# A first projection group on rows that are not yet normed

## The chip, the cores and the metric

The kernel runs on one core of one Trainium2 chip. Its metric is the device time of one execution in microseconds (us). A core has five engines that run side by side, each through its own instructions in order: TensorE (PE, matrix products into PSUM), VectorE (DVE), ScalarE (ACT), GpSimd (POOL) and SyncE (SP, which here only issues transfers). They wait for each other by semaphores. Weights and inputs come from HBM by DMA.

## The reference

Two transformer blocks on 256 tokens of width 2048, in float32. The first is a conformer convolution block with an MLP, the second mixes two kinds of attention and has an MLP of its own. The change lies in the first lines of the first block:

```python
def rms_norm(x, g):
    xf = x.astype(jnp.float32)
    y = xf * lax.rsqrt(jnp.mean(xf * xf, axis=-1, keepdims=True) + NORM_EPS)
    return (y * g.astype(jnp.float32)).astype(x.dtype)

def conformer_conv(h, w_pw1, b_pw1, w_dw, b_dw, ln_g, ln_b, w_pw2, b_pw2):
    u = h @ w_pw1 + b_pw1                       # h = rms_norm(x, norm_mix_g), 2048 -> 4096
    a, gate = jnp.split(u, 2, axis=-1)
    u = a * jax.nn.sigmoid(gate)
    u = depthwise_conv(u, w_dw) + b_dw          # 31 taps along the tokens, one filter per channel
    u = jax.nn.silu(layer_norm(u, ln_g, ln_b))
    return u @ w_pw2 + b_pw2

h = x + conformer_conv(rms_norm(x, norm_mix_g), ...)
h = h + square(relu(rms_norm(h, norm_ffn_g) @ w_up)) @ w_down
h = rms_norm(h, final_norm_g)
# second block: rmsnorm, projections, stick-breaking and forgetting attention, output
# projection, rmsnorm, squared-relu MLP, final rmsnorm
```

1/rms is one number per token, so it can stand ahead of the projection or behind it: (r * x * g) @ W is r * ((x * g) @ W).

## The kernel before

**Exact products.** Every float32 operand of a matrix product is split into `hi`, a rounded copy that TensorE takes at its fast rate, and `lo`, the rest. A product is hi*hi + hi*lo + lo*hi. For weights, `split(i)` has ScalarE cast `raw` to `hi` (L127) and VectorE or GpSimd subtract to get `lo` (L128): VectorE for steps 0 to 4, GpSimd for later projection steps. For activations `split_act` does the same (L178, L179).

**Steps.** The program is a list of steps, one unit of weights of 1 MB each. `emit` writes them out in order: for step i it first issues loads (three units ahead, three `raw` buffers) and splits (one unit ahead up to step 2, two ahead from step 3 on), then the step's matmuls, and then whatever earlier steps have deferred by a number of steps (`run_pending`). For the first 40 steps the order so written is the order of every engine's queue.

**Stage 1.** The pointwise projection goes in groups of two channel blocks (`groups`), for each of which a step takes a quarter of the 2048 inputs: steps 0 to 3 are group 0 with quarters kq = 0 to 3, steps 4 to 7 group 1, and so on. A step has 48 matmuls into the PSUM tile `pw` (L518, L520, L521). The activations of quarter kq are the tile `xa[kq]`: 4 blocks of 128 channels, hi and lo, 256 tokens. The same four tiles serve all groups. Behind the last quarter `glu` gates the result (ScalarE's sigmoid `sg`, VectorE's product `u_p`, ScalarE's copy `u`), and `conv(gi)` is deferred so that it comes behind the first step of the next group: some of the 31 taps of each channel block on TensorE (`ca`, with diagonal matrices `dg` that ScalarE makes), the others on VectorE, 54 multiply-adds for group 0 (L394), the sum into `xs_t` (L406). Layer norm follows after all groups.

**The start.** `prologue` loads x into `res` (two tiles of 128 tokens), has ScalarE square it (L208) and takes 1/rms (`rstd_of`). Quarter c of x, here chunk c, then goes through `first_a` (ScalarE and VectorE multiply by 1/rms into `xn`, TensorE transposes into `pt`) and `first_b` (VectorE multiplies by the gain into `xf`, L307; `split_act` into `xa[c]`), both called from `split`. `vectors`, in step 2, transposes the small vectors and the filters.

Of the kernel before, what the change touches and what calls it, by code (L numbers as in the profile page):

```python
# [10 lines left out]
AF = mybir.ActivationFunctionType  # L11
# [4 lines left out]
P = 128  # L16
# [17 lines left out]
def kernel(  # L34
# [31 lines left out]

    state = {}

# [1 line left out]
    ident = const.tile([P, P], F32, name="ident")  # L70
    ones = const.tile([P, P], F32, name="ones")
    ones_c = const.tile([P, P], F32, name="ones_c")
# [17 lines left out]
        nc.scalar.dma_start(out=t, in_=bass.AP(tensor=v.tensor, offset=v.offset, ap=[[0, P], [1, D]]))  # L90
        return t

# [1 line left out]
    steps = []  # L94

    def unit_std(w, r0, c0):
# [15 lines left out]
    def split(i):  # L112
        if callable(steps[i][0]):
            parts[i] = steps[i][0]()
            return
        srcs, eng = steps[i][0]
        if i < 4:
            for c in ((0, 1), (), (2,), (3,))[i]:
                first_a(c)
            first_b(i)  # L120
        raw = raws.pop(i)
        hi = wpool.tile([P, D], F32R, tag="hi", name=f"hi{i}")
        lo = wpool.tile([P, D], F32R, tag="lo", name=f"lo{i}")
        e = nc.gpsimd if eng == "p" and i > 4 else nc.vector
        n = D if i else D // 2
        for j in range(0, D, n):
            nc.scalar.copy(hi[:, j:j + n], raw[:, j:j + n])  # L127
            e.tensor_tensor(out=lo[:, j:j + n], in0=raw[:, j:j + n], in1=hi[:, j:j + n].bitcast(F32), op=ALU.subtract)  # L128
        k = srcs[0][0]
        parts[i] = (hi.rearrange("p (k c) -> p k c", k=k), lo.rearrange("p (k c) -> p k c", k=k))  # L130

# [41 lines left out]

    mm = nc.tensor.matmul

# [1 line left out]
    def split_act(src, hi, lo):  # L177
        nc.scalar.copy(hi, src)  # L178
        nc.vector.tensor_tensor(out=lo, in0=src, in1=hi.bitcast(F32), op=ALU.subtract)  # L179
# [52 lines left out]
                mm(ps[h], xh, lo[:, k, :], start=False, stop=False)  # L232
                mm(ps[h], xl, hi[:, k, :], start=False, stop=(last and k == 3))  # L233

# [1 line left out]
    s1 = ExitStack()  # L236
    p1 = s1.enter_context(tc.tile_pool(name="stage1", bufs=1))
    cpool = s1.enter_context(tc.tile_pool(name="cpool", bufs=4))
# [1 line left out]
    def prologue():  # L240
        nc.vector.memset(col[:, 0:1], 1.0)
        nc.vector.memset(col[:, 1:2], EPS1)
        nc.vector.memset(col[:, 2:3], EPS2)
        nc.vector.memset(col[:, 3:4], 0.0)
        nc.scalar.preload_act_table_set(LOG_EXP)
        for h in range(2):
            for j in range(2):
                nc.sync.dma_start(out=res[:, h, j * 1024:(j + 1) * 1024],
                                  in_=x[h * P:(h + 1) * P, j * 1024:(j + 1) * 1024])
        make_identity(nc, ident)  # L250
        vab = xpool.tile([P, 3, P], F32, tag="xt", name="vab")
        va, vb, vm = (vab[:, i, :] for i in range(3))
        wdr = xpool.tile([P, D], F32, tag="xt", name="wdr")[0:KT, :]
        nc.scalar.dma_start(out=vm[0:16, :], in_=norm_mix_g.rearrange("(k p) -> k p", p=P))
        for i, g in enumerate((norm_ffn_g, g_attn, g_mlp, final_norm_g, b_dw, ln_g, ln_b)):
            nc.gpsimd.dma_start(out=va[16 * i:16 * i + 16, :], in_=g.rearrange("(k p) -> k p", p=P))
        nc.gpsimd.dma_start(out=vb[0:32, :], in_=b_pw1.rearrange("(k p) -> k p", p=P))
        nc.gpsimd.dma_start(out=vb[32:40, :], in_=g_out_sb.rearrange("(k p) -> k p", p=P))
        nc.gpsimd.dma_start(out=vb[40:48, :], in_=g_out_fox.rearrange("(k p) -> k p", p=P))
        nc.gpsimd.dma_start(out=wdr, in_=w_dw)  # L260
        state["raw_vectors"] = va, vb, wdr
        ss0 = new_ss("ss0")
        for h in range(2):
            for j in range(2):
                for c in range(2):
                    sumsq(ss0, h, 2 * j + c)
        r = rstd_of(ss0, EPS1, "r0")
        state["r0"], state["xa"] = r, [xt_tile(f"xa{c}") for c in range(4)]
        pm = ps1([P, 16], "pm")
        nc.tensor.transpose(pm, vm[0:16, :], ident[0:16, 0:16])  # L270
        nc.vector.tensor_copy(vt[:, G_MIX:G_MIX + 16], pm)
        nc.vector.memset(ones, 1.0)
# [11 lines left out]
                nc.tensor.transpose(pw[:, k, 0:KT], wdr[:, cb * P:(cb + 1) * P], ident[:KT, :KT])  # L284
            nc.vector.tensor_copy(wd[:, 8 * q:8 * q + 8, 0:KT], pw[:, :, 0:KT])

    def first_a(c):
        r, pts = state["r0"], []
        for h in range(2):
            xn = wk([P, 512], "xn")  # L290
            src = res[:, h, c * 512:(c + 1) * 512]
            if h == 0:
                nc.scalar.activation(out=xn, in_=src, func=AF.Copy, scale=r[:, h:h + 1])
            else:
                nc.vector.tensor_scalar(out=xn, in0=src, scalar1=r[:, h:h + 1], scalar2=None, op0=ALU.mult)
            pt = ps1([P, 4, P], f"pt{h}{c}")
            for k in range(4):
                nc.tensor.transpose(pt[:, k, :], xn[:, k * P:(k + 1) * P], ident)
            pts.append(pt)
        state["pts", c] = pts  # L300

    def first_b(c):
        g = vt[:, G_MIX + 4 * c:G_MIX + 4 * c + 4].unsqueeze(2).to_broadcast([P, 4, P])
        xfs, xt = [], state["xa"][c]
        for h, pt in enumerate(state.pop(("pts", c))):
            xf = wk([P, 4, P], "xf")
            nc.vector.tensor_tensor(out=xf, in0=pt, in1=g, op=ALU.mult)  # L307
            xfs.append(xf)
        for h, xf in enumerate(xfs):
            split_act(xf, xt[:, :, 0, h * P:(h + 1) * P], xt[:, :, 1, h * P:(h + 1) * P])  # L310

    def late_constants():
        rowbc = bcast_rows(b_pw2, "bpw2")
# [16 lines left out]
        for h in range(2):  # L330
            nc.gpsimd.tensor_tensor(out=res[:, h, :], in0=res[:, h, :], in1=rowbc, op=ALU.add)

# [1 line left out]
    xs_t = p1.tile([P, NB, T], F32, name="xs_t")  # L334
    u_t = [p1.tile([P, 2, T + 2 * PAD], F32, name=f"u{i}") for i in range(2)]
    acc0 = p1.tile([P, T], F32, name="acc0")
# [6 lines left out]
    def glu(gi, ps):  # L343
        cbs = groups[gi]
        u = u_t[gi % 2]
        state["u_p", gi] = []
        for i, cb in enumerate(cbs):
            sg = wk([P, T], "sg")
            nc.scalar.activation(out=sg, in_=ps[:, 2 + i, :], func=AF.Sigmoid, bias=vcol(B_PW1, 16 + cb))
            up = ps1([P, 512], "u_p")  # L350
            nc.vector.memset(up[:, 0:PAD], 0.0)
            nc.vector.memset(up[:, T + PAD:T + 2 * PAD], 0.0)
            nc.vector.scalar_tensor_tensor(out=up[:, PAD:PAD + T], in0=ps[:, i, :], scalar=vcol(B_PW1, cb),
                                           in1=sg, op0=ALU.add, op1=ALU.mult)
            nc.scalar.copy(u[:, i, PAD:PAD + T], up[:, PAD:PAD + T])
            state["u_p", gi].append(up)
# [138 lines left out]
    def stage1_group(gi):  # L495
        cbs = groups[gi]
        if len(cbs) == 2:
            for kq in range(4):
                c0 = cbs[0] * P
                unit = ([(4, 512, 0, w_pw1[kq * 512:(kq + 1) * 512, c0:c0 + 256]),  # L500
                         (4, 512, 256, w_pw1[kq * 512:(kq + 1) * 512, D + c0:D + c0 + 256])], "p")

                def fn(hi, lo, kq=kq):
                    if kq == 0:
                        state["pw1"] = ps2([P, 4, T], f"pw1_{gi}")
                    if gi == 0 and kq == 2:
                        vectors()
                    if kq == (3 if gi == 0 else 0):
                        state["dg", gi] = diags(gi)
                    if gi == 1 and kq == 0:  # L510
                        late_constants()
                    ps, xt = state["pw1"], state["xa"][kq]
                    for m in range(4):
                        for k in range(4):
                            wh, wl = hi[:, k, m * P:(m + 1) * P], lo[:, k, m * P:(m + 1) * P]
                            first = kq == 0 and k == 0
                            last = kq == 3 and k == 3
                            mm(ps[:, m, :], wh, xt[:, k, 0, :], start=first and m % 2 == 0, stop=False,  # L518
                               skip_group_check=True)
                            mm(ps[:, m, :], wh, xt[:, k, 1, :], start=False, stop=False, skip_group_check=True)  # L520
                            mm(ps[:, m, :], wl, xt[:, k, 0, :], start=False, stop=last, skip_group_check=True)  # L521
                    if kq == 3:
                        glu(gi, ps)
                        defer(2, lambda: conv(gi))
                step(unit, fn)
# [34 lines left out]
                            add_bias_rows()  # L560
                step(unit, fn)

# [1 line left out]
    def post_chunk(c, ss, gain, xts, delay):  # L564
        for h in range(2):
            sumsq(ss, h, c)
# [40 lines left out]
            srcs, _ = unit_std(w_pw2, q * 512, c * 512)  # L607
            step((srcs, "p" if q == 0 and c < 2 or (q, c) == (1, 0) else "v"), fn)

# [1 line left out]
    def ffn(w_u, w_d, tail):  # L611
        NG = FF // 512

# [78 lines left out]
            defer(2, spread)  # L692
        defer(1, rate)

# [1 line left out]
    s2 = ExitStack()  # L696

    def open_attention():
# [70 lines left out]
        state["lr"] = lr  # L769

    def attention(kind, grp, qk, v, mt):
        """Four heads: list of steps, each emitted in order with the projections between."""
        ap = state["ap"]
        qT, kT = qk
        per_pair = []
# [196 lines left out]
                eng = nc.sync if j == 0 else nc.scalar  # L972
                eng.dma_start(out=out[h * P:(h + 1) * P, j * 1024:(j + 1) * 1024], in_=v)

# [1 line left out]
    for gi in range(len(groups)):  # L976
        stage1_group(gi)
    pw2()
# [54 lines left out]
```

## Time and profile before

| | |
|---|---|
| median of 3 runs | 2202.88 us (2202.71 to 2204.14) |
| span of the profiled execution | 2200.8 us |
| TensorE busy | 2166.2 us, 98% of the span |
| VectorE, ScalarE, GpSimd busy | 65%, 44%, 8% |
| read from HBM | 391.53 MB |

The profiled execution has no time of its own beside its span, which goes from its first to its last instruction; the runs' times are 2.1 us above it (median). In the profile L127 is line 127 of the kernel; `PE` is TensorE's matmuls, `PEld` its weight loads; a group of instructions is written as line, engine, operation, `out<-in` and shape. `[0.86 <-PE pw L521]` is the idle time ahead of an instruction on its engine and what ended it. A row of a stretch gives its start and end, its length, the busy time and count of each engine, the granted share of TensorE's clock, the DMA share and GB/s.

### The profile page before, as it was taken

To read this page: it belongs to the slowest core of one execution; us is meant where nothing else is said; L and a number is where in the kernel's file an instruction comes from. 1 tells how busy PE (TensorE), PEld (TensorE's weight loads), DVE (VectorE), ACT (ScalarE), POOL (GpSimd) and SP (SyncE) were. 2 spreads that over 40 slices of the span, in tenths; PEclk is the share of its full clock that TensorE was granted. 3 is DMA by queue.
4 is the path that set the end of the run, shared out by engine and by line. 5 is a ranking of instruction groups with operands and counts; after the bars stand their busy time and mean duration, and the time that the engine had idled before them with its cause. 6 is when DMAs were issued, how large, how long until landed. Compare 5 with 4: busy or idle time off the path is not lost.

```text
span 2200.8 us, 27600 instructions
## 1 busy us (share of the span) xinstructions
PE 2166.2 (98%) x11521; PEld 1861.1 (85%) x11521; DVE 1436.8 (65%) x1648; ACT 958.8 (44%) x965; POOL 175.2 (8%) x88
## 2 busy tenths in 40 slices
PE   7999899999999999999999999999999999999998
PEld 7999778888888888888788888888888888888886
DVE  5997775666655666566866565676656665666656
ACT  6455454434333433343645454544333433343333
POOL 2886500000000000000000000000000000000000
PEclk9999999999999999999999999999999999999999
DMA  7555155555555555556544554455555555555553
GB/s 227 164 170 150 63 193 187 186 188 188 190 191 191 184 198 191 191 174 221 177 156 153 172 172 159 166 172 191 192 189 187 186 190 189 191 189 192 191 191 134
DMA packets 219612, 395.41 MB, mean 180 GB/s; under 512 B 8993, under 2 KB 46017, under 8 KB 219073
## 3 DMA queue, kind: packets, MB, share of 16 engines
q1 hardware_dynamic: 216160, 389.05, 54.6%
q10 hardware_dynamic: 2960, 4.27, 0.6%
q8 instruction: 90, 1.47, 0.3%
q0 software_dynamic: 368, 0.34, 0.1%
q14 instruction: 34, 0.28, 0.0%
HBM read 391.53 MB, written 2.10 MB: 179 GB/s over the span
## 4 chain that ended last, share of the span: by engine, by line
PE 97%; ACT 1%; DVE 1%; issue 0%; DMA 0%; ACTq 0%; SPq 0%; DVEq 0%
PE up L222 22%; PE dn L231 11%; PE dn L233 11%; PE dn L232 11%; PE up L224 10%; PE pj L222 5%; PE pj L224 3%; PE pw L521 2%; PE pw L518 2%; PE pw L520 2%; PE ca L386 2%; PE wo L232 1%; PE wo L233 1%; PE wo L231 1%; PE pv L233 1%; PE pv L231 1%
## 5 line engine op out<-in xcount | busy, mean ns | idle before, releaser
L128 DVE TENSOR_TENSOR lo<-raw,hi 128x2048 fp32r<-128x2048 f32 (+1 forms) x339 | 774.3, 2285 | 585.6 <-ACT hi L127 585.6
L127 ACT CAST hi<-raw 128x2048 fp32r<-128x2048 f32 (+1 forms) x369 | 702.8, 1906 | 935.9 <-PE up L222 340.3
L222 PE MATMUL up<-xn,hi 128*128 128x512 f32 x2048 | 718.3, 398 | 0.0
L224 PE MATMUL up<-xn,lo 128*128 128x256 f32 x1920 | 539.4, 281 | 0.0
L222 PEld LDWEIGHTS up<-xn,hi 128*128 128x128 f32 x2048 | 378.2, 188 | 83.8
L231 PE MATMUL dn<-hi,act 128*128 128x512 f32 x1024 | 398.8, 389 | 0.0
L233 PE MATMUL dn<-hi,act 128*128 128x512 f32 x1024 | 398.4, 389 | 0.0
L232 PE MATMUL dn<-lo,act 128*128 128x512 f32 x1024 | 398.3, 389 | 0.0
L224 PEld LDWEIGHTS up<-xn,lo 128*128 128x128 f32 x1920 | 362.5, 189 | 5.9
L641 DVE SCALAR_TENSOR_TENSOR res<-dn,rsq,res 128x512 f32<-128x512 f32 x256 | 191.4, 748 | 57.9 <-PE dn L233 57.9
L232 PEld LDWEIGHTS dn<-lo,act 128*128 128x128 f32 x1024 | 192.3, 188 | 40.1
L233 PEld LDWEIGHTS dn<-hi,act 128*128 128x128 f32 x1024 | 192.2, 188 | 40.1
L231 PEld LDWEIGHTS dn<-hi,act 128*128 128x128 f32 x1024 | 192.2, 188 | 38.6
L222 PE MATMUL pj<-xn,hi 128*128 128x512 f32 x512 | 179.7, 398 | 0.0
L394 DVE SCALAR_TENSOR_TENSOR acc<-u_p,wd,acc 128x256 f32<-128x256 f32 x385 | 151.6, 478 | 0.0
L128 POOL TENSOR_TENSOR lo<-raw,hi 128x2048 fp32r<-128x2048 f32 x30 | 138.5, 4620 | 85.6 <-ACT hi L127 85.6
L224 PE MATMUL pj<-xn,lo 128*128 128x256 f32 x480 | 134.5, 280 | 0.0
L518 PE MATMUL pw<-xa,hi 128*128 128x256 f32 x448 | 129.1, 288 | 0.7 <-ACT hi L127 0.7
L521 PE MATMUL pw<-xa,lo 128*128 128x256 f32 x448 | 127.6, 285 | 0.9 <-DVE lo L128 0.9
L520 PE MATMUL pw<-xa,hi 128*128 128x256 f32 x448 | 127.5, 285 | 0.0
L222 PEld LDWEIGHTS pj<-xn,hi 128*128 128x128 f32 x512 | 94.5, 188 | 20.6 <-DVE q_t L906 0.5
L224 PEld LDWEIGHTS pj<-xn,lo 128*128 128x128 f32 x480 | 90.6, 189 | 1.5
(259 smaller groups left out, 2033.5 us busy)
## 6 DMA issues: line engine op xcount, KB each, us to landing
raw<-in_ffn_w_up_dram SPq DMA_DIRECT2D x64, 1024.0 KB, 5.2
raw<-in_ffn_w_down_dram SPq DMA_DIRECT2D x64, 1024.0 KB, 5.1
raw<-in_w_up_dram SPq DMA_DIRECT2D x64, 1024.0 KB, 5.3
raw<-in_w_down_dram SPq DMA_DIRECT2D x64, 1024.0 KB, 5.0
raw<-in_w_in_dram SPq DMA_DIRECT2D x48, 1024.0 KB, 5.1
raw<-in_conv_w_pw_dram SPq DMA_DIRECT2D x64, 512.0 KB, 4.8
raw<-in_conv_w_pw_dram SPq DMA_DIRECT2D x16, 1024.0 KB, 5.1
raw<-in_w_out_dram SPq DMA_DIRECT2D x16, 1024.0 KB, 5.1
```

The costliest lines, as they stand in the source:

```text
L127: nc.scalar.copy(hi[:, j:j + n], raw[:, j:j + n])
L128: e.tensor_tensor(out=lo[:, j:j + n], in0=raw[:, j:j + n], in1=hi[:, j:j + n].bitcast(F32), op=ALU.subtract)
L222: mm(o, wh, xt[:, k, :, :], start=(kq == 0 and k == 0), stop=last)
L224: mm(o[:, 0:T], wl, xt[:, k, 0, :], start=False, stop=False, skip_group_check=True)
L231: mm(ps[h], xh, hi[:, k, :], start=(first and k == 0), stop=False)
L232: mm(ps[h], xh, lo[:, k, :], start=False, stop=False)
L233: mm(ps[h], xl, hi[:, k, :], start=False, stop=(last and k == 3))
L394: nc.vector.scalar_tensor_tensor(out=acc[k], in0=src, scalar=w, in1=acc[k], op0=ALU.mult, op1=ALU.add)
L518: mm(ps[:, m, :], wh, xt[:, k, 0, :], start=first and m % 2 == 0, stop=False, skip_group_check=True)
L520: mm(ps[:, m, :], wh, xt[:, k, 1, :], start=False, stop=False, skip_group_check=True)
L521: mm(ps[:, m, :], wl, xt[:, k, 0, :], start=False, stop=last, skip_group_check=True)
L641: nc.vector.scalar_tensor_tensor(out=r, in0=ps[h], scalar=state["rsq"][:, h:h + 1], in1=r, op0=ALU.mult, op1=ALU.add)
```

## The change

x is loaded in chunks of 512 columns, with the weights of steps 0 to 2 between them on the same queue. `first_chunk` transposes a chunk straight from `res`, multiplies by the gain into `xs_t` (which is free until conv writes it) and splits it into `xa[c]`; so `xa` holds x * g without 1/rms. Group 0 is projected on that. The sums of squares follow the weights' casts on ScalarE. After step 2 `row_scales` takes 1/rms, spreads it over the partitions by a diagonal matrix and a product with ones, and keeps it in `delta`. `glu(0)` multiplies the projection's PSUM by `delta`. For the groups after it `scale_chunk(c)`, at the head of `split(4 + c)`, multiplies the chunk in `xs_t` by `delta` and splits it into `xa[c]` again. Step 0 takes all products with `hi` ahead of those with `lo`.

```diff
@@ split
         if i < 4:
-            for c in ((0, 1), (), (2,), (3,))[i]:
-                first_a(c)
-            first_b(i)
+            first_chunk(i)
+        elif i < 8:
+            scale_chunk(i - 4)
         raw = raws.pop(i)
...
             e.tensor_tensor(out=lo[:, j:j + n], in0=raw[:, j:j + n], in1=hi[:, j:j + n].bitcast(F32), op=ALU.subtract)
+        if i < 4:
+            for h in range(2):
+                sumsq(state["ss0"], h, i)
@@ prologue
-        for h in range(2):
-            for j in range(2):
-                nc.sync.dma_start(out=res[:, h, j * 1024:(j + 1) * 1024],
-                                  in_=x[h * P:(h + 1) * P, j * 1024:(j + 1) * 1024])
+        for c in range(4):
+            for h in range(2):
+                nc.sync.dma_start(out=res[:, h, c * 512:(c + 1) * 512], in_=x[h * P:(h + 1) * P, c * 512:(c + 1) * 512])
+            if c < 3:
+                load(c)
+        at["load"] = 3
...
-        ss0 = new_ss("ss0")
-        for h in range(2):
-            for j in range(2):
-                for c in range(2):
-                    sumsq(ss0, h, 2 * j + c)
-        r = rstd_of(ss0, EPS1, "r0")
-        state["r0"], state["xa"] = r, [xt_tile(f"xa{c}") for c in range(4)]
+        state["ss0"], state["xa"] = new_ss("ss0"), [xt_tile(f"xa{c}") for c in range(4)]
@@ first_a and first_b give way to
+    def first_chunk(c):
+        g = vt[:, G_MIX + 4 * c:G_MIX + 4 * c + 4].unsqueeze(2).to_broadcast([P, 4, P])
+        xt = state["xa"][c]
+        for h in range(2):
+            pt = ps1([P, 4, P], f"pt{h}{c}")
+            for k in range(4):
+                nc.tensor.transpose(pt[:, k, :], res[:, h, (4 * c + k) * P:(4 * c + k + 1) * P], ident)
+            nc.vector.tensor_tensor(out=xs_t[:, 4 * c:4 * c + 4, h * P:(h + 1) * P], in0=pt, in1=g, op=ALU.mult)
+        for h in range(2):
+            tok = slice(h * P, (h + 1) * P)
+            split_act(xs_t[:, 4 * c:4 * c + 4, tok], xt[:, :, 0, tok], xt[:, :, 1, tok])
+
+    def row_scales():
+        r = rstd_of(state["ss0"], EPS1, "r0")
+        pr = ps1([P, T], "pr0")
+        for h in range(2):
+            dgr = wk([P, P], "dgr")
+            nc.vector.tensor_scalar(out=dgr, in0=ident, scalar1=r[:, h:h + 1], scalar2=None, op0=ALU.mult)
+            mm(pr[:, h * P:(h + 1) * P], ones, dgr, start=True, stop=True)
+        nc.scalar.copy(delta, pr)
+
+    def scale_chunk(c):
+        v = xs_t[:, 4 * c:4 * c + 4, :]
+        nc.vector.tensor_tensor(out=v, in0=v, in1=delta.unsqueeze(1).to_broadcast([P, 4, T]), op=ALU.mult)
+        xt = state["xa"][c]
+        split_act(v, xt[:, :, 0, :], xt[:, :, 1, :])
@@ glu
+        if gi == 0:
+            for m in (2, 0):
+                v = ps[:, m:m + 2, :]
+                nc.vector.tensor_tensor(out=v, in0=v, in1=delta.unsqueeze(1).to_broadcast([P, 2, T]), op=ALU.mult)
@@ stage1_group, in a step's function
+                    if gi == 0 and kq == 0:
+                        for k in range(4):
+                            for m in range(4):
+                                wh = hi[:, k, m * P:(m + 1) * P]
+                                mm(ps[:, m, :], wh, xt[:, k, 0, :], start=k == 0 and m % 2 == 0, stop=False,
+                                   skip_group_check=True)
+                                mm(ps[:, m, :], wh, xt[:, k, 1, :], start=False, stop=False, skip_group_check=True)
+                        for k in range(4):
+                            for m in range(4):
+                                mm(ps[:, m, :], lo[:, k, m * P:(m + 1) * P], xt[:, k, 0, :], start=False, stop=False,
+                                   skip_group_check=True)
+                        return
...
+                    if gi == 0 and kq == 2:
+                        row_scales()
```

What this does to the order of the queues shows at three places. First the transfers on SyncE at the start, before (`res` is x, each `raw` one unit of weights):

```order
L248 DMA res<-in_x_dram 128x1024 x4
L109 DMA raw_166<-in_conv_w_pw_dram 128x4x256 x2
L109 DMA raw_169<-in_conv_w_pw_dram 128x4x256 x2
L109 DMA raw_172<-in_conv_w_pw_dram 128x4x256 x2
L109 DMA raw_217<-in_conv_w_pw_dram 128x4x256 x2
```

and now:

```order
L251 DMA res<-in_x_dram 128x512 x2
L109 DMA raw_107<-in_conv_w_pw_dram 128x4x256 x2
L251 DMA res<-in_x_dram 128x512 x2
L109 DMA raw_112<-in_conv_w_pw_dram 128x4x256 x2
L251 DMA res<-in_x_dram 128x512 x2
L109 DMA raw_117<-in_conv_w_pw_dram 128x4x256 x2
L251 DMA res<-in_x_dram 128x512 x2
L109 DMA raw_179<-in_conv_w_pw_dram 128x4x256 x2
```

x, which came whole ahead of all weights, now comes in four parts with a unit of weights behind each.

Second, VectorE from the gate of group 0 to that of group 1, before (`u_p` the gated product, `acc` the taps of conv(0), L406 its sum):

```order
L353 SCALAR_TENSOR_TENSOR u_p<-pw_0_235,vt,sg 128x256
L399 TENSOR_SCALAR acc<-u_p,wd 128x256 x2
L394 SCALAR_TENSOR_TENSOR acc<-u_p,wd,acc 128x256 x54
L406 SCALAR_TENSOR_TENSOR xs_t<-ca_625,vt,acc 128x256 x2
L351 MEMSET u_p 128x15
L352 MEMSET u_p 128x15
L353 SCALAR_TENSOR_TENSOR u_p<-pw_1_553,vt,sg 128x256
```

and now (`xa_143` is the tile of chunk 2, `xa_144` that of chunk 3):

```order
L360 SCALAR_TENSOR_TENSOR u_p<-pw_0_209,vt,sg 128x256
L311 TENSOR_TENSOR xs_t<-xs_t,delta 128x1024
L182 TENSOR_TENSOR xa_143<-xs_t,xa_143 128x4x256
L406 TENSOR_SCALAR acc<-u_p,wd 128x256 x2
L401 SCALAR_TENSOR_TENSOR acc<-u_p,wd,acc 128x256 x54
L413 SCALAR_TENSOR_TENSOR xs_t<-ca_624,vt,acc 128x256 x2
L311 TENSOR_TENSOR xs_t<-xs_t,delta 128x1024
L182 TENSOR_TENSOR xa_144<-xs_t,xa_144 128x4x256
```

The rescaling of chunk 2 stands ahead of conv(0), that of chunk 3 behind its 58 instructions.

Third, ScalarE from the copy of `u` in group 0 to the first sigmoid of group 1, before (`hi_692` is the weights of step 7):

```order
L355 COPY u_91<-u_p 128x256
L127 CAST hi_546<-raw_387 128x2048
L367 ACTIVATE dg_554<-ident,wd 128x128 x4
L367 ACTIVATE dg_559<-ident,wd 128x128 x2
L90 DMA bpw_562<-in_conv_b_pw_dram 128x2048
L127 CAST hi_692<-raw_466 128x2048
L127 CAST hi_747<-raw_473 128x2048
```

and now (`hi_694` is the weights of step 7):

```order
L362 COPY u_91<-u_p 128x256
L181 CAST xa_143<-xs_t 128x4x256
L127 CAST hi_545<-raw_357 128x2048
L374 ACTIVATE dg_553<-ident,wd 128x128 x4
L374 ACTIVATE dg_558<-ident,wd 128x128 x2
L90 DMA bpw_561<-in_conv_b_pw_dram 128x2048
L181 CAST xa_144<-xs_t 128x4x256
L127 CAST hi_694<-raw_457 128x2048
L127 CAST hi_749<-raw_467 128x2048
```

The cast of chunk 3 stands ahead of the cast of step 7's weights; on GpSimd the order is the same in both, lo of step 7 behind those of steps 5 and 6.

More of the change, by code (lines that the diff above doesn't have):

```diff
@@ L285, in vectors @@
             nc.vector.tensor_copy(wd[:, 8 * q:8 * q + 8, 0:KT], pw[:, :, 0:KT])
-    def first_a(c):
-        r, pts = state["r0"], []
+    def first_chunk(c):
+        g = vt[:, G_MIX + 4 * c:G_MIX + 4 * c + 4].unsqueeze(2).to_broadcast([P, 4, P])
+        xt = state["xa"][c]
         for h in range(2):
[L290 to L295, printed above, removed]
             pt = ps1([P, 4, P], f"pt{h}{c}")
             for k in range(4):
[L298 to L310, printed above, removed]
+                nc.tensor.transpose(pt[:, k, :], res[:, h, (4 * c + k) * P:(4 * c + k + 1) * P], ident)
[16 more added lines that the diff above has]
+        split_act(v, xt[:, :, 0, :], xt[:, :, 1, :])
     def late_constants():
```

## The prediction

> **What bounds the kernel now.** I read the page's head and its chain of waits first, then the waits of TensorE, then the first 80 us by stretches and instruction by instruction on the engines that the change touches.
>
> ```profile
> span 2200.8 us, 27600 instructions
> PE 2166.2 (98%) x11521; PEld 1861.1 (85%) x11521; DVE 1436.8 (65%) x1648; ACT 958.8 (44%) x965; POOL 175.2 (8%) x88
> PE 97%; ACT 1%; DVE 1%; issue 0%; DMA 0%; ACTq 0%; SPq 0%; DVEq 0%
> ```
>
> TensorE is the bound almost everywhere: 34.6 us of the span are not its own. The change can win only in that remainder, so the next view is where it lies. Stretches (core, PE, PEld, DVE, ACT, POOL busy, then granted clock, DMA share, GB/s), and the waits of TensorE from 20 to 80 us:
>
> ```profile
> 0.00:5.00 5.00, 0.25 (x1) 0.18 (x1) 0.15 (x4) 1.49 (x2) 4.19 (x13) 1.00 0.61 186
> 5.00:10.00 5.00, 0.00 (x0) 0.00 (x0) 0.00 (x0) 4.34 (x13) 2.27 (x6) 1.00 1.02 329
> 10.00:15.00 5.00, 1.48 (x7) 1.48 (x8) 2.06 (x10) 2.97 (x8) 1.43 (x4) 1.00 1.11 328
> 15.00:20.00 5.00, 3.50 (x19) 2.86 (x17) 4.43 (x6) 3.13 (x4) 0.00 (x0) 1.00 0.93 275
> ...
> 17.20:20.60 3.40, 1.75 (x10) 1.34 (x11) 3.15 (x4) 1.64 (x2) 0.00 (x0) 1.00 0.69 216
> 20.60:24.00 3.40, 3.40 (x18) 3.40 (x18) 2.20 (x5) 3.08 (x4) 0.00 (x0) 0.50 0.72 219
> ...
> 56.00:73.40 17.40, 17.40 (x147) 17.40 (x146) 17.38 (x46) 4.04 (x4) 16.62 (x13) 1.00 0.58 187
> ```
> ```profile
> PE pw L521 <- DVE lo L128: 0.2, 1, 0.2
> ```
>
> The reader is to see two things. TensorE starts late: it has next to nothing until 13.5 us, and from 20.3 us (up to 80, where this view ends) it waits no more. That late start is what the change goes after. And from 56.0 to 73.4 us VectorE is busy for 17.38 of 17.40 us beside a full TensorE: VectorE has no room there either. The three steps in that stretch, 144 matmuls, give 0.12 us a matmul and 5.8 us a step of 48.
>
> The rows that set the lockstep, from the timeline (start, length):
>
> ```profile
> 47.77 0.47 ACT L349 ACTIVATE sg<-pw,vt 128x256 f32<-128x256 f32 x1 [0.86 <-PE pw L521]
> 50.35 1.02 DVE L399 TENSOR_SCALAR acc<-u_p,wd 128x256 f32<-128x256 f32 x2
> 51.28 21.24 DVE L394 SCALAR_TENSOR_TENSOR acc<-u_p,wd,acc 128x256 f32<-128x256 f32 x54
> 72.43 0.87 DVE L406 SCALAR_TENSOR_TENSOR xs_t<-ca,vt,acc 128x256 f32<-128x256 f32 x2
> 67.56 1.91 ACT L127 CAST hi<-raw 128x2048 fp32r<-128x2048 f32 x1 [3.84 <-PE pw L520]
> 73.39 0.47 ACT L349 ACTIVATE sg<-pw,vt 128x256 f32<-128x256 f32 x1 [3.92 <-PE pw L521]
> 52.72 4.60 POOL L128 TENSOR_TENSOR lo<-raw,hi 128x2048 fp32r<-128x2048 f32 x1 [4.19 <-ACT hi L127]
> ```
>
> Step 3 ends on TensorE by 47.77 us (the first sigmoid waits for it), VectorE's share of conv(0) runs from 50.35 to 73.30, 22.95 us, and step 7 ends at 73.39. VectorE and TensorE finish a group together. Whatever is put on VectorE's queue behind conv(0) and ahead of step 7 is therefore late for TensorE.
>
> **The change, part by part.** Everything is timed on the profiled execution (span 2200.8 us); the median of the runs, 2202.88, is 2.1 above that span, and I carry that over.
>
> *Start.* The transposes no longer wait for 1/rms. In the old order these rows set the start:
>
> ```profile
> 4.79 0.63 ACT L208 ACTIVATE junk<-res 128x512 f32<-128x512 f32 x1 [2.71 <-DMA res<-in_x_dram]
> 8.27 0.63 ACT L208 ACTIVATE junk<-res 128x512 f32<-128x512 f32 x1 [0.50 <-DMA res<-in_x_dram]
> 13.52 3.68 PE L298 MATMUL pt<-ident,xn 128*128 128x128 f32 x16 [9.23 <-ACT xn L293]
> 17.94 0.39 PE L518 MATMUL pw<-xa,hi 128*128 128x256 f32 x1 [0.74 <-ACT hi L127]
> ```
> ```profile
> L128 DVE TENSOR_TENSOR lo<-raw,hi 128x2048 fp32r<-128x2048 f32 x4 | 9.2, 2290 | 3.3 <-ACT hi L127 3.3
> L307 DVE TENSOR_TENSOR xf<-pt,vt 128x512 f32<-128x512 f32 x8 | 5.3, 688 | 2.1 <-PE pt L298 2.0
> L128 DVE TENSOR_TENSOR lo<-raw,hi 128x1024 fp32r<-128x1024 f32 x2 | 2.4, 1222 | 0.3 <-ACT hi L127 0.3
> L285 DVE COPY wd<-pw 128x248 f32<-128x248 f32 x2 | 0.7, 406 | 0.0
> L127 ACT CAST hi<-raw 128x2048 fp32r<-128x2048 f32 x9 | 17.1, 1905 | 11.7 <-PE pw L520 11.7
> L178 ACT CAST xa<-xf 128x512 fp32r<-128x512 f32 x8 | 4.9, 620 | 10.3 <-DVE xf L307 10.2
> L127 ACT CAST hi<-raw 128x1024 fp32r<-128x1024 f32 x2 | 2.0, 1042 | 0.0
> ```
>
> The queue carries the same bytes in another order: chunk 0 of x (0.52 MB), weights 0 (1.05 MB), chunk 1, and so on. A first 0.52 MB had landed at 4.79 and 1.57 MB at 8.27, so chunk 0 is there at 4.8 and weights 0 at 8.3; at 329 GB/s chunk 1 follows at 9.8, weights 1 at 13.0, chunk 2 at 14.6, and at the 275 GB/s of the next stretch weights 2 at 18, chunk 3 at 20, weights 3 at 24. But TensorE's order has the transposes of chunk 1 ahead of step 0, so step 0 waits for 9.8, not 4.8. Half of 3.68 us for 8 transposes: step 0 starts at 11.7 (hi 0 is done at 10.4, two casts of 1.04) against 17.94. It needs 5.8 us, and 1.7 more because the clock was 0.50 for 3.40 us soon after the first dense work: 19.2. Transposes of chunk 2 (1.0), step 1: 26.0.
>
> I found no wait for data there; what paces it is VectorE and ScalarE in turn. Chunk 3 is transposed from 26.0, its first half at 26.6; two gains (0.69 each), casts of both halves (to 28.65), hi 3 (1.9), lo 3 (2.29): 32.9. The copies of the vectors, 1.0 together: 33.9. Then the row scales. The same helpers run later in the old kernel:
>
> ```profile
> 1091.37 0.16 DVE L199 TENSOR_REDUCE rs_a<-ss 128x2 f32<-128x8 f32 x1
> 1093.37 0.71 PE L687 MATMUL pr<-dgr,ones 128*128 128x128 f32 x4 [0.38 <-DVE dgr L686]
> 1094.11 0.37 ACT L689 COPY rb<-pr 128x256 f32<-128x256 f32 x1
> ```
>
> From the reduce to the copy's end that is 3.1 us; delta is ready at 37.0. The sums of squares (0.63 a half chunk, some 0.75 with the read-out) sit on ScalarE behind hi 3 and end at 32, under lo 3: nothing, while lo 3 covers them. TensorE is through with step 2 before that (26.0, transposes, 5.8), waits for the row scales, begins step 3 behind their matmuls at 36.6 and ends it at 42.4: a lead of 5 us over 47.8. That is all the start yields.
>
> *Rescaling.* Each chunk adds on VectorE a multiply of 128x1024 and a subtraction of that size, on ScalarE a cast, one waiting for the other. The multiply is not in the trace: from below the 1.22 of the subtraction of this size, from above twice the 0.69 of the gain multiply; I take 1.22, the same operands in SBUF. From delta, along the order of the two queues:
>
> ```profile
> 43.74 1.86 ACT L367 ACTIVATE dg<-ident,wd 128x128 f32<-128x128 f32 x6
> 45.62 1.28 ACT L349 ACT_TABLE_LOAD   x1
> 48.27 0.49 DVE L353 SCALAR_TENSOR_TENSOR u_p<-pw,vt,sg 128x256 f32<-128x256 f32 x1 [4.83 <-ACT sg L349]
> ```
>
> Chunk 0: multiply 1.22, cast 1.04; hi 4 1.9; lo 4 2.29; chunk 1: 1.22, cast 1.04; hi 5 1.9 (the cast of chunk 1 and hi 5 stand ahead of conv(0)'s diagonals); diagonals 1.86; table load 1.28; the gate pair twice, 0.47 + 0.49, with a copy of the size of the one at 1094.11 (0.37) between, 2.3; chunk 2: 1.22 + 1.04 + 1.22. Together 19.5, and 0.4 for hand-offs: conv(0) starts on VectorE at 56.9, not 50.35. The two multiplies of the projection's PSUM by delta (0.69 each, by the gain multiply that reads PSUM at this size, at most twice that) fall under diagonals and table load; without that cover they would cost 1.4 to 2.8.
>
> *The wait that is new.* Chunk 3 is rescaled in the preparation of step 7, which comes behind conv(0). So: conv(0) 22.95 to 79.9; multiply 1.22; cast 1.04; hi 7, which stands behind that cast on ScalarE, 1.9; lo 7 on GpSimd 4.6: 88.6. Before, hi 7 and lo 7 were done while conv(0) ran. TensorE reaches step 7 at about 68 and has nothing else to take: 20 us of wait. Behind it on ScalarE wait hi 8, hi 9 and the next sigmoid, on GpSimd lo 8 and lo 9, but these stay ahead of TensorE (lo 8 at 93.2).
>
> *Restart.* What a gap does to the clock the old trace shows at the layer norm:
>
> ```profile
> PE pp L231 <- ACT y L178: 6.4, 1, 6.4
> 263.00:270.00 7.00, 4.96 (x11) 3.27 (x12) 6.76 (x13) 6.19 (x10) 0.30 (x1) 0.51 0.00 1
> ```
>
> After 6.4 us without work it ran 4.96 busy us at 0.51, so half of that is lost: 2.4 us. Step 7 ends at 88.6 + 5.8 + 2.4 = 96.8, against 73.39.
>
> *Sum.* 96.8 - 73.4 = 23.4 us. From there on each group is as before, and conv(1) starts right behind step 7 in both, so nothing gives it back. Span 2224.2, time 2226.3; I say 2226.
>
> The Trainium skill, TensorE: Matmul & The Clock Gate, Part 1, says the array halves its clock after one idle window of about 3.4 us and gets it back after one busy window. By that the restart costs 1.7 us and the time is 2225.6; the trace, with 4.96 us at half clock, agrees in kind and is longer. Its Part 4 says that transposes do not count as activity, which would leave step 0 slow from its first matmul. The trace differs: after 3.68 us of transposes the clock stood at 1.00 from 17.20 on. By the page the 1.7 us in step 0 is certain; by the row it may be absent, and the time is then 2224.6.
>
> **Rivals.** *The start's gain survives (faster).* The place is step 7 too: if chunk 3 got its scale before conv(0) took VectorE, TensorE would keep the lead of 5 us: 2202.9 - 5 = 2198. The point from which it decides is delta at 37.0 less 23, 14 us; but chunk 3 only lands at 20. Against it also stands the order of VectorE's queue. *Lead and wait cancel (same).* Conv(0)'s late start, 6.5 us, takes the lead back and no more: 2203 to 2204. It needs chunk 3 off the path, for which nothing speaks. *The chain is half hidden.* ScalarE and VectorE overlap better than the row-by-row sum, the wait is 8 to 14 us shorter: 2212 to 2217. *GpSimd loses its lead.* It was busy 16.62 of 17.40 us; if each lo comes just in time after step 7, one more lo, 4.6 us and then some, is paid: 2231 to 2236.
>
> **How the numbers follow.** The likeliest case 0.80; half hidden 0.08; GpSimd 0.05; faster 0.04; same 0.03. The bounds: delta at 35.3 if the clock does not halve (-1.7), no half clock at the restart (-2.4), shorter hand-offs and the rest of the start (-4) give 2218; the multiplies at the upper bound on four chunks (0.6), start rows later by 2 and one lo give 2233. I set 2217 to 2232. Slower by over 0.2% (about what a measurement of this kernel can tell from no change, 4.4 us): 0.80 + 0.08 + 0.05 = 0.93; faster 0.04; same 0.03.
>
> **What would show it.** In the profile after: TensorE's first projection matmul near 11.7; step 3's end near 42; the first conv row of VectorE near 57; a wait of some 20 us of TensorE at the projection, released by GpSimd's lo or ScalarE's hi; the next sigmoid near 97; the clock at 0.5 in the 4 us before that; the layer norm some 23 us later than now. It is wrong if step 7 does not wait, or if a later wait in stage 1 gives the time back.

## The result and the profile after

The changed kernel takes 2225.11 us (median of 4 runs, 2224.15 to 2225.96) against 2203.04 for the kernel before: ratio 1.0098, 95% interval 1.0085 to 1.0112. It is slower by 22.1 us; the span of its profiled execution is longer by 21.6.

The page of the changed kernel, its head, the engines and the chain that ended last:

```profile
span 2222.4 us, 27617 instructions
...
PE 2170.8 (98%) x11525; PEld 1864.0 (84%) x11525; DVE 1446.3 (65%) x1656; ACT 960.3 (43%) x966; POOL 174.9 (8%) x88
...
PE 94%; issue 2%; DVE 2%; ACT 1%; POOL 1%; DMA 0%; SPq 0%; ACTq 0%; POOLq 0%; DVEq 0%
```

TensorE did nearly the same work; its busy time is 4.6 us longer. It still bounds the kernel, but its share of the chain fell from 97% to 94%. What it waited for in the first 320 us (engine, tile and line, what it waited for, us in total, times, longest):

```profile
PE pw L537 <- ACT hi L127: 15.7, 1, 15.7
PE pp L234 <- ACT y L181: 6.4, 1, 6.4
PE pw L540 <- POOL lo L128: 4.6, 2, 3.8
...
PE ca L393 <- ACT u L362: 3.1, 1, 3.1
PE pr L306 <- DVE dgr L305: 1.1, 1, 1.1
...
PE pw L540 <- DVE lo L128: 0.9, 1, 0.9
```

The 6.4 at `pp` is the layer norm's and was there before. The 15.7 and the 3.8 are new; both are waits of step 7, one for its `hi`, one for its `lo`. Together they are 19.5 of the 21.6 us. The waits of 3.1 and 0.9 us and the rest of the 4.6 (0.8, at step 6) lie between step 3 and step 7. They use up the lead that the start gives: it is some 6 us at step 3's end (41.31 against 47.8 for the old sigmoid, which starts some 0.4 us behind the last matmul) and under 1 us at step 7. Four stretches around the start and that wait:

```profile
10.00:15.00 5.00, 5.00 (x25) 4.92 (x24) 4.46 (x6) 4.27 (x8) 0.95 (x2) 1.00 1.07 328
15.00:20.00 5.00, 5.00 (x42) 5.00 (x42) 2.87 (x2) 1.97 (x5) 0.00 (x0) 1.00 1.09 356
...
70.00:80.00 10.00, 0.00 (x0) 0.00 (x0) 9.53 (x23) 0.43 (x1) 0.00 (x0) 0.50 0.00 0
80.00:90.00 10.00, 3.74 (x15) 3.44 (x16) 1.37 (x3) 6.01 (x4) 7.51 (x2) 0.50 0.16 51
```

From 10 to 20 us TensorE is now full, where it was busy 4.98 us of 10 before: the early start is real. From 70 to 80 us it does nothing, ScalarE and GpSimd next to nothing, and no byte moves, because the three weight buffers wait too. VectorE alone is busy. Which of its instructions these are, and what stands behind them, the timeline shows (start, length, engine, line, operation, and in brackets the idle time ahead of it with what ended it):

```profile
35.59 0.37 ACT L307 COPY delta<-pr 128x256 f32<-128x256 f32 x1 [1.84 <-PE pr L306]
...
55.60 0.87 DVE L406 TENSOR_SCALAR acc<-u_p,wd 128x256 f32<-128x256 f32 x2
56.38 21.23 DVE L401 SCALAR_TENSOR_TENSOR acc<-u_p,wd,acc 128x256 f32<-128x256 f32 x54
77.53 0.87 DVE L413 SCALAR_TENSOR_TENSOR xs_t<-ca,vt,acc 128x256 f32<-128x256 f32 x2
78.32 1.22 DVE L311 TENSOR_TENSOR xs_t<-xs_t,delta 128x1024 f32<-128x1024 f32 x1
79.56 1.04 ACT L181 CAST xa<-xs_t 128x1024 fp32r<-128x1024 f32 x1 [21.56 <-DVE xs_t L311]
80.52 5.49 ACT L127 CAST hi<-raw 128x2048 fp32r<-128x2048 f32 x3
...
82.49 13.62 POOL L128 TENSOR_TENSOR lo<-raw,hi 128x2048 fp32r<-128x2048 f32 x3 [19.31 <-ACT hi L127]
...
94.39 0.47 ACT L356 ACTIVATE sg<-pw,vt 128x256 f32<-128x256 f32 x1 [8.38 <-PE pw L540]
```

Conv(0) holds VectorE from 55.60 to 78.40. Chunk 3's multiply comes right behind; its cast on ScalarE waited 21.56 us for it; hi 7 stands behind that cast, and GpSimd's lo 7 behind hi 7 (it had been idle 19.31 us). TensorE has what it needs at 87.06, and the sigmoid that ends step 7 comes at 94.39 instead of 73.39: +21.0, about the 19.5 of the wait and the 1.5 of half clock behind it. The last 0.6 us of the span come at the layer norm. There the clock stays at 0.50 for 5.86 busy us, in the kernel before for 4.75; half of the difference is 0.55. The stretch at half clock in the changed kernel:

```profile
281.66:291.90 10.24, 5.86 (x13) 3.95 (x14) 8.70 (x18) 8.78 (x14) 1.20 (x1) 0.50 0.00 1
```

And in the kernel before:

```profile
262.96:269.79 6.83, 4.75 (x10) 3.11 (x11) 6.59 (x14) 6.02 (x10) 0.09 (x1) 0.50 0.00 1
```

### The profile page after: what moved, and what is told of

Same layout as the page of the kernel before. It is cut to its first block, busy times and chain, and to the rows that moved or that the text cites. A ratio compares the mean times of both kernels' runs of the same rounds, so it can differ in the third digit from the quotient of the medians.

```text
span 2222.4 us, 27617 instructions
## 1 busy us (share of the span) xinstructions
PE 2170.8 (98%) x11525; PEld 1864.0 (84%) x11525; DVE 1446.3 (65%) x1656; ACT 960.3 (43%) x966; POOL 174.9 (8%) x88
## 4 chain that ended last, share of the span: by engine, by line
PE 94%; issue 2%; DVE 2%; ACT 1%; POOL 1%; DMA 0%; SPq 0%; ACTq 0%; POOLq 0%; DVEq 0%
PE up L225 22%; PE dn L234 10%; PE dn L236 10%; PE dn L235 10%; PE up L227 10%; PE pj L225 5%; PE pj L227 3%; PE pw L540 2%; PE pw L539 2%; PE pw L537 2%; PE ca L393 2%; PE wo L236 1%; PE wo L235 1%; PE wo L234 1%; PE pv L236 1%
## 5 line engine op out<-in xcount | busy, mean ns | idle before, releaser
L537 PE MATMUL pw<-xa,hi 128*128 128x256 f32 x432 | 124.8, 289 | 15.7 <-ACT hi L127 15.7
L539 PE MATMUL pw<-xa,hi 128*128 128x256 f32 x432 | 123.0, 285 | 0.0
L537 PEld LDWEIGHTS pw<-xa,hi 128*128 128x128 f32 x432 | 83.7, 194 | 16.1 <-ACT hi L127 15.9
```

## The experiments

The theories: the *queue theory*, step 7 waits because chunk 3's rescaling stands behind conv(0) on VectorE; the *load theory*, the added VectorE and ScalarE work is too much wherever it stands; the *start theory*, the new start itself costs. All edits are on the changed kernel, except the rescaling alone, which is on the kernel before.

**Chunk 3 ahead of conv(0).** It is rescaled right behind chunk 2.

```diff
-        elif i < 8:
+        elif i < 7:
             scale_chunk(i - 4)
+            if i == 6:
+                scale_chunk(3)
```

> Chunk 3 is rescaled right behind chunk 2, ahead of conv(0) on VectorE's queue. The queue theory (step 7 waits because chunk 3 stands behind the 23 us of conv(0)): the wait of 15.7 and 3.8 us at step 7 goes to about 1 us. Conv(0) starts 3.5 us later, at 59.1, and ends at 82.0, so the copy of u that the taps of conv(1) on TensorE need is 4.4 us later than in the kernel before: time about 2207 (2206 to 2211 with some half clock). Rival, the load theory (the added rescaling work costs what it costs wherever it stands): the same work is there, time stays near 2225. Rival, the start theory (the new start is itself the loss): 2225 as well.

Measured: 2207.25 us, ratio 1.0018 (1.0010 to 1.0027). TensorE's waits:

```profile
PE ca L395 <- ACT u L364: 3.1, 1, 3.1
PE pw L542 <- POOL lo L130: 2.5, 1, 2.5
...
PE pr L308 <- DVE dgr L307: 1.1, 1, 1.1
...
PE pw L542 <- DVE lo L130: 0.9, 1, 0.9
```

The wait at step 7 is gone, and of the 22.1 us 4.1 are left, with the same instructions, chunk 3's moved ahead of conv(0)'s 58. The kernel is still slower than before, so the start's gain is spent elsewhere, and not where I expected it: the taps of conv(1) do not wait, and that the time is the expected 2207 is luck. TensorE waits for conv(0)'s `u`, which ScalarE and VectorE make late (3.1), for a `lo` of GpSimd whose `hi` came late (2.5), and twice its clock halves:

```profile
51.77:55.20 3.43, 3.43 (x11) 2.68 (x9) 2.32 (x4) 1.42 (x2) 0.00 (x0) 0.50 0.92 292
...
65.43:68.84 3.41, 3.41 (x19) 3.41 (x18) 3.41 (x9) 0.00 (x0) 3.41 (x5) 0.50 0.87 292
```

These stretches begin 0.8 and 1.4 us behind the ends of the two waits. Full of work at half clock, each costs 1.7. So the waits of 3.1 and 2.5 us cost some 3.4 us more than their length, if the spells are theirs, as the order in time suggests. In the changed kernel the same wait of 3.1 us left the clock at 1.00 (last section), so such a spell does not come with every wait.

**Step 7's weights first.** Chunk 3 keeps its place behind conv(0); hi 7 and lo 7 are written ahead of it.

```diff
-        elif i < 8:
+        elif i < 7:
             scale_chunk(i - 4)
...
             e.tensor_tensor(out=lo[:, j:j + n], in0=raw[:, j:j + n], in1=hi[:, j:j + n].bitcast(F32), op=ALU.subtract)
+        if i == 7:
+            scale_chunk(3)
```

> In the preparation of step 7 the weights are split first and chunk 3 is rescaled after them; all the work and its place behind conv(0) stay. Queue theory: hi 7 and lo 7 run under conv(0), and step 7 starts when chunk 3 has its multiply, cast and lo: 78.3 + 1.2 + 1.0 + 1.2 = 81.8 instead of 87.1, time about 2220. Load theory and start theory: no change, 2225.

Measured: 2218.44 us, ratio 1.0068 (1.0056 to 1.0081). TensorE's waits at step 7:

```profile
PE pw L539 <- ACT xa L183: 13.2, 1, 13.2
...
PE pw L541 <- DVE xa L184: 0.7, 1, 0.7
```

TensorE now waits for the chunk itself, 13.9 us instead of 19.5. The wait has two parts, as the queue theory has it: conv(0) holds chunk 3, and chunk 3's cast holds the weights of step 7.

**The rescaling alone.** The kernel before, with its old start; x arrives normed, and the four chunks, kept in `xs_t` as in the change, are multiplied by a `delta` of ones and split again.

```diff
+        elif i < 8:
+            scale_chunk(i - 4)
...
+        nc.vector.memset(delta, 1.0)
```

> The kernel before, with its old start, and only the four rescalings added where the change has them, by a delta of ones (a factor of one, set at the beginning). Queue theory: with delta at hand from the beginning the chain begins behind the vectors' copies at 41.0; conv(0) starts at about 61 and ends at 84, step 7 starts at 93 and ends at 100 instead of 73.4: time about 2230, later than with the new start, since the old start is 5 us later. Load theory (each rescaling costs its own 3.5 us): about 2217. Start theory (the new start makes the loss): 2203.

Measured: 2229.20 us, ratio 1.0117 (1.0101 to 1.0133). TensorE's waits at step 7:

```profile
PE pw L527 <- ACT hi L129: 15.9, 2, 15.2
...
PE pw L530 <- POOL lo L130: 3.8, 1, 3.8
```

And the sigmoid of group 1, in the timeline:

```profile
99.41 0.47 ACT L358 ACTIVATE sg<-pw,vt 128x256 f32<-128x256 f32 x1 [9.05 <-PE pw L530]
```

The same two waits at step 7 with the old start. The start theory (2203) falls: the new start brings that sigmoid from 99.41 to 94.39, 5 us to the good. The load theory's 2217 falls too.

**The start alone.** The changed start and the row scales, without `scale_chunk` and without the multiply in `glu`.

```diff
-        elif i < 8:
-            scale_chunk(i - 4)
...
-        if gi == 0:
-            for m in (2, 0):
-                ...
```

> The new start without any scaling: 1/rms is still taken and spread, but neither chunks nor PSUM are multiplied by it (that part of the computation is left out). Queue theory: only the lead of the start is left, 6.1 us at step 3: time about 2197. Load theory: the same. Start theory: 2203 or slower, since x in four parts between the weights gives nothing.

Measured: 2196.11 us, ratio 0.9969 (0.9957 to 0.9981). The sigmoid of group 1:

```profile
65.91 0.47 ACT L350 ACTIVATE sg<-pw,vt 128x256 f32<-128x256 f32 x1 [3.93 <-PE pw L534]
```

At 65.91 against 73.39 the start is worth 7.5 us in the profile, 7.0 in the medians. In the changed kernel nearly all of it is lost ahead of step 7, and the wait there comes on top. Against this run the changed kernel takes 29.0 us more, and the one with chunk 3 ahead of conv(0) 11.1 more. So chunk 3's place is worth 17.9 of the 29.0 us. The other 11.1 us the scaling costs even with chunk 3 ahead, which the queue theory as worded here does not cover.

**Scale at the gate.** No chunk is rescaled. All groups are projected on x * g, and every group's PSUM is multiplied by `delta`.

```diff
-        elif i < 8:
-            scale_chunk(i - 4)
...
-        if gi == 0:
-            for m in (2, 0):
-                v = ps[:, m:m + 2, :]
+        n = len(cbs)
+        for m in (2, 0):
+            v = ps[:, m:m + n, :]
...
```

> No chunk is rescaled; every group's gate multiplies its PSUM by 1/rms, as group 0 does: nine times two multiplies of 0.72 us on VectorE in place of four rescalings. Queue theory: nothing stands behind conv(0), TensorE keeps its start (step 3 ends at 41.6 instead of 47.7), VectorE takes 26.3 us a group against TensorE's 25.7 but may lag by some 4 us before a tap waits: time about 2197 (2196 to 2200). Load theory: 13 us of multiplies on VectorE, which was full in stage 1: 2203 to 2212. Start theory: 2203 or more.

Measured: 2200.36 us, ratio 0.9987 (0.9979 to 0.9996), a little faster than both kernels, but 4.2 us behind the start alone, where I had expected about 1 (2197, at most 2200). The gates of groups 0 and 1 on VectorE:

```profile
42.20 1.43 DVE L351 TENSOR_TENSOR pw<-pw,delta 128x512 f32<-128x512 f32 x2 [1.25 <-PE pw L538]
70.15 1.43 DVE L351 TENSOR_TENSOR pw<-pw,delta 128x512 f32<-128x512 f32 x2
```

And TensorE's waits:

```profile
PE pp L232 <- ACT y L179: 7.2, 1, 7.2
...
PE lne L448 <- DVE xs_t L411: 1.4, 1, 1.4
...
PE ca L391 <- ACT u L360: 0.9, 2, 0.6
```

The multiplies cost VectorE 1.43 us a group. VectorE was already as full as TensorE in a group, so it falls behind and the layer norm at the end of stage 1 starts later: 7.22 and 1.42 us of wait, 6.36 and 0.58 with the start alone. That is 1.7 of the 4.2; half of it, the growth at `pp`, is an add on GpSimd (last section).

**Scale at the gate, two refinements.** One runs the row scales' matmuls and their copy (now in `spread_scales`) in the middle of step 3 and writes conv(0)'s diagonals behind the first gate:

```diff
...
+                        if gi == 0 and kq == 3 and m == 1:
+                            spread_scales()
...
+                        if gi == 0:
+                            state["dg", gi] = diags(gi)
```

> The scaling at every gate (2200.4), with two waits taken out: the two matmuls that spread 1/rms stand in the middle of step 3 instead of ahead of it, and the diagonals of group 0 are made after its gate instead of before. TensorE loses the wait of 1.1 us, VectorE starts conv(0) some 2 us earlier and the taps of conv(2) and conv(3) on TensorE no longer wait 0.6 and 0.3 us. If these waits are what the version loses: about 2198.5. If the time beyond the start alone (2196.1) is lost at the end of stage 1, at the layer norm: 2199 to 2200.

Measured: 2199.20 us, ratio 0.9984 (0.9975 to 0.9993). The wait at the row scales is gone, the layer norm's 7.2 and 1.5 stay, and the time lies in the second reading's range, 2199 to 2200, but too near the first's 2198.5 to decide. The other refinement is a probe: it multiplies in groups 0 to 6 only, to see what the last two groups, of one channel block each, cost the layer norm:

```diff
-        for m in (2, 0):
+        for m in (2, 0) if gi < 7 else ():
```

> The scaling at the gates of the seven groups of two channel blocks; the last two groups, of one block each, are left unscaled (that part of the computation is left out). If the two multiplies of the last gate stand on the path to the layer norm (the wait there was 1.4 and 7.2 us instead of 0.6 and 6.4): about 1.7 us less than 2200.4, 2198.7. If the time is lost in the groups before: 2200.4 again.

Measured: 2199.56 us, ratio 0.9985 (0.9976 to 0.9994). The wait of `lne` falls from 1.4 to 0.6, that of `pp` from 7.2 to 7.0, and the time by 0.8: between the two readings, so it decides for neither. The three intervals overlap, so that either refinement is a gain over the plain form isn't shown. The first has the lowest median of the three: 2199.20 us, 3.7 less than the kernel before and 26 less than the changed kernel.

## Why the prediction was right, and which terms were off

The predicted time was 2226.0 us; the mechanism, the place and the order of its parts are in the trace as they were forecast. By its own steps:

- **The start.** Step 0's first matmul at 11.02 (11.7 predicted), step 3's end at 41.31 (42.4), against 47.77 before, where the sigmoid marks it. Its half clock was taken as 1.7; TensorE's rows show more. The first and the last matmul at half clock, and the first at full:

```profile
9.40 1.97 PE L293 MATMUL pt<-ident,res 128*128 128x128 f32 x8 [2.89 <-DMA res<-in_x_dram]
11.02 0.56 PE L524 MATMUL pw<-xa,hi 128*128 128x256 f32 x1
...
15.22 0.38 PE L526 MATMUL pw<-xa,hi 128*128 128x256 f32 x1
15.43 0.28 PE L524 MATMUL pw<-xa,hi 128*128 128x256 f32 x1
```

  They stand 0.21 us apart up to 15.43 and 0.12 after, although the clock's column of the stretch from 10 to 15 us reads 1.00; there the spacing is the better witness. These are 20 matmuls at 0.094 us more each, 1.9 us. I had placed the slow spell behind the first dense work, as in the kernel before; here the clock is low from the first matmul on. The Trainium skill, TensorE: Matmul & The Clock Gate, Part 4, says that transposes do not count as activity in the way that matmuls do, and this start, taken by itself, would agree. In the kernel before, for which the prediction had read 1.00 from 17.20 on in that column, matmuls did stand 0.12 us apart at 19.5 us with hardly anything but transposes ahead of them, so the rule is not settled by this case.
- **The row scales.** `delta` was ready at 35.96, 37.0 predicted. TensorE waited 1.1 for them.
- **The chain from delta to conv(0).** 19.9 us with its hand-offs predicted, 35.96 to 55.60 = 19.6 measured. The multiply of a chunk, which no row had shown, took 1.22, as taken. The PSUM multiplies took 1.43 for the two, as taken, under ScalarE's diagonals and table load. Missed: conv(0)'s taps on TensorE wait 3.1 us for `u`, which this chain delays. It costs nothing here, since TensorE would have waited at step 7 all the same; with chunk 3 ahead it is a main part of what is left.
- **The wait.** TensorE was there at 66.77 (68) and had lo 7 at 87.06 (88.6): 19.5 us of wait, 20 predicted. That the length fits is luck, since the 68 is not what the prediction's terms give: 42.4, three steps of 5.8 and the taps (12 matmuls, 2.6 us in the kernel before) come to 62.4, and a fourth step makes 68. TensorE came as late as 66.77 because of the three waits on its way (3.1, 0.9 and 0.8 us), which the prediction does not have. The sum is not touched, as it goes by when lo 7 is there. Here the 1.5 us are the earlier `delta` (1.0), the chain (0.3) and conv(0), 22.80 for 22.95.
- **The restart.** This is the mis-sized term: 2.4 us predicted, from the layer norm's stretch. Step 7 took 7.3 us from 87.06 to the sigmoid instead of 5.8, so 1.5. By the Trainium skill, TensorE: Matmul & The Clock Gate, Part 1, the full clock comes back after one busy window of about 3.4 us; the estimate from that, 1.7 us, was nearer. The layer norm is no good measure of a restart: TensorE has little work there, and its spell at half clock holds 4.75 busy us before and 5.86 after. That spell's growth, 0.55 us, I had not foreseen.
- **The sum.** +23.4 predicted at the sigmoid of group 1, +21.0 measured; the span was predicted 1.8 too long. The profiled execution of the changed kernel was the shortest of its four runs, so the median lies 2.7 above its span instead of 2.1; by that luck the time was off by 0.9 only.
- **The rivals.** The start's gain is there (7.0 us, by the start alone) and did not survive. Lead and wait cancel almost, 2207.25, once chunk 3 is off the path: the condition I had named for it, and it was met by an edit only. GpSimd kept its lead behind step 7: lo 8 and lo 9 follow lo 7 in one run of 13.62 us, and TensorE waits for neither. The chain was not half hidden.

What stays open: 2.5 of the 4.2 us between scaling at the gate and the start alone. The taps' waits of 0.9 us in the rows above are likely a part. In the two profiles the start itself differs too (below): conv(0)'s taps begin at 47.76 against 45.85, without a wait for them in either. I made no run that takes this out.

## What to carry to other kernels

An operation that is cheap by its length is priced by what stands ahead of it on its queue and by what stands behind its result: here 1.2 us of VectorE behind 22.8 us of taps, with a cast and a step's weights behind it, made a wait of 19.5 us. When work is pulled ahead of a normalisation, put the scale where no other engine's next input hangs on it (in the gate, behind the product), and look at the step in which the two busiest engines finish together before adding anything to either. A wait of 3 us of TensorE can cost more than its length: behind the taps' wait of some 3 us its clock halved in three of the four profiles that have it, but not in the changed kernel's.

## What the runs showed of the hardware that I had not expected

*The clock's return at the start is not tied to the work alone.* The start alone has the changed kernel's instructions up to there and begins within 0.1 us of it:

```profile
9.47 2.02 PE L291 MATMUL pt<-ident,res 128*128 128x128 f32 x8 [2.84 <-DMA res<-in_x_dram]
11.14 0.56 PE L518 MATMUL pw<-xa,hi 128*128 128x256 f32 x1
...
12.78 0.32 PE L520 MATMUL pw<-xa,hi 128*128 128x256 f32 x1
12.94 0.28 PE L518 MATMUL pw<-xa,hi 128*128 128x256 f32 x1
```

It is at full clock from 12.9 us, the changed kernel from 15.4, scaling at the gate (which begins 0.8 later) from 16.3. The two edits that move chunk 3 have the same start as well, and 13.8 and 14.3 us. The spread of 3.4 us is one spell at half clock in length and worth up to 1.7 us in any one execution: a difference of that size between two profiles need not be the effect of an edit.

*The same wait halves the clock in one execution and not in another.* The taps of conv(0) wait 3.1 us for `u` in the changed kernel and with chunk 3 ahead of conv(0). The 12 matmuls behind that wait, in this order:

```profile
51.37 2.87 PE L393 MATMUL ca<-u,dg 128*128 128x256 f32 x12 [3.10 <-ACT u L362]
...
50.95 4.54 PE L395 MATMUL ca<-u,dg 128*128 128x256 f32 x12 [3.12 <-ACT u L364]
```

They take 2.87 us at a granted clock of 1.00, and 4.54 us at 0.50 for most of it. The clock halved too behind the taps' wait with step 7's weights first (3.1 us) and with the rescaling alone (2.7 us). The spells shown in this document last 3.43, 3.41, 6.83 and 10.24 us, that is one, two and three times one length, and the two of the first experiment begin 13.66 us apart, four times it. So it may matter whether a wait falls into one such stretch or is split between two; that is worked out from these lengths, and no run tests it.

*An add on GpSimd holds up a product on VectorE.* At the layer norm VectorE squares `delta` in SBUF, 128x256, while GpSimd adds a bias to `res`. With the start alone:

```profile
251.70 1.42 DVE L454 TENSOR_TENSOR ln_t<-delta 128x256 f32<-128x256 f32 x1 [1.77 <-ACT delta L452]
...
254.62 0.42 DVE L192 TENSOR_TENSOR ln_t<-lnr 128x256 f32<-128x256 f32 x1 [0.26 <-ACT lnr L457]
...
243.66 9.18 POOL L332 TENSOR_TENSOR res<-res,bpw 128x2048 f32<-128x2048 f32 x2
```

With the gate's multiplies in groups 0 to 6:

```profile
255.04 2.04 DVE L458 TENSOR_TENSOR ln_t<-delta 128x256 f32<-128x256 f32 x1 [1.77 <-ACT delta L456]
...
247.62 9.17 POOL L332 TENSOR_TENSOR res<-res,bpw 128x2048 f32<-128x2048 f32 x2
```

The product takes 0.42 us when GpSimd is idle, and here 1.42 and 2.04: it ends at 253.12 and 257.08, 0.3 us after GpSimd's add in both (252.84 and 256.79). The Trainium skill, SBUF — State Buffer, Who interferes with whom, says that a VectorE instruction with two inputs in SBUF is blocked for the whole of a GpSimd instruction that reads SBUF and started first; the trace agrees. So the layer norm goes on when that add ends: 1.0 and 1.6 us of its wait lie there. With the multiplies at every gate it is 2.28 us:

```profile
256.63 2.28 DVE L458 TENSOR_TENSOR ln_t<-delta 128x256 f32<-128x256 f32 x1 [1.77 <-ACT delta L456]
```

That is 0.86 more than with the start alone, as much as the wait at `pp` grew (7.22 for 6.36 us). A kernel with the add in another place was not run.
